# Output weights of an attention layer gated and split earlier and kept in DRAM, and two kinds of vector additions done by accumulating DMAs

## The chip, the cores and the metric

The kernel runs on one core of one Trainium2 chip. The metric is the device time of one launch in microseconds (us); the time of a kernel is the median of several runs. The engines of the core are named as the profile names them: PE is TensorE (matrix products; PEld is its loading of weights), DVE is VectorE, ACT is ScalarE, POOL is GpSimd, SP is SyncE, which here only issues DMAs. Operands lie in SBUF as tiles of 128 partitions, sums of products in PSUM, everything larger in DRAM.

## The reference, cut to what matters

Two layers of a decoder trunk work on x of 1024 rows (SEQ) by 1024 (D_MODEL) in float32. Each layer is a token mixer followed by a squared-ReLU MLP of width 4096; each of the four sub-layers is `x <- LayerNorm(ALPHA * x + gate * f(x * (1 + scale) + shift))`, where shift, scale and gate come from a condition vector. The first mixer is a gated MLP over chunks; the second, which the change is about, is an attention of 16 heads of 64 in three dilated patterns:

```python
B_PATTERNS = ((128, 1), (512, 4), (2048, 16))       # window, dilation
def mixer_b(h, w_qkv, w_out, slopes):
    qkv = (h @ w_qkv).reshape(B, S, N_PAT, 3, B_HEADS, B_HEAD_DIM)
    for g, (window, dilation) in enumerate(B_PATTERNS):
        o, lse = dilated_branch(qkv[:, :, g, 0], qkv[:, :, g, 1], qkv[:, :, g, 2],
                                window, dilation, slopes)
        outs.append(o)
        lses.append(lse)
    wts = jax.nn.softmax(jnp.stack(lses, axis=0), axis=0)[..., None]
    o = jnp.sum(wts * jnp.stack(outs, axis=0), axis=0)
    return o.reshape(B, S, B_HEADS * B_HEAD_DIM).astype(h.dtype) @ w_out
...
        y = mixer_b(h, b_w_qkv[j], b_w_out[j], slopes)
        x = layer_norm(ALPHA * x + gate * y, ln_g[i, 0], ln_b[i, 0])
```

`dilated_branch` is a causal softmax attention inside a window with a linear bias (ALiBi). So per position and head there are three outputs and three log-sums `lse`; the softmax over the three gives the weights with which the outputs are added, and the sum is multiplied with `w_out`.

## The kernel before, in words

**Numbers and products.** A float32 operand is split into a high and a low part that the array takes: `split` (L102, L103) copies to the high part on ACT and forms source minus high part on DVE. Each product is then three matmuls (high by high, high by low, low by high).

**Stages.** After mixer A and its MLP comes `values`, then `attention`, and then the MLP of layer 1. `values` runs over the 35 entries of `V_STEPS`, each a pattern `g`, a kind `X` (0 and 1 are q and k of the undilated pattern g=0, 2 is v) and one of the seven products `p` of a Strassen-like scheme, in the order 1, 2, 5, 6, 7, 4, 3. Each step makes four sums `m` of 12 matmuls each. `evict` (L1215) takes the finished sums: products 1, 5 and 6 are only copied; after the other four the result is split into a tile of pool `parted`, tag `vs`, which has two buffers, and stored by a POOL DMA, q and k to `qk_dram` (L1229), v to `v_dram` (L1234). The right-hand weights of a step are loaded by SP one to two steps ahead (L1099).

**Attention.** `attention` (L1272) treats pairs of heads, 8 of them, and in each pair the patterns 2, 1, 0: 24 groups in a fixed order, with 8 slots each and two positions in a slot. Work is put at a position by `at(slot, position)`; the program is then written out position by position. Between the positions it writes a stream of projections, `project()` (L1358: q and k of the dilated patterns), by a credit. In a group the scores (L1447) get their bias and row maximum in a DVE operation (L1467) and their exponential on ACT (L1469), are transposed (L1500, L1503) and split (pThi on ACT, pTlo on DVE), and a slot and a half later multiplied with v (L1527). The outputs are gathered in a tile `oT`, half by an ACT copy (L1536) and half by a DVE one (L1537); the tag `oT` has four buffers. The biases are made by POOL (L1435), a group ahead.

**Merge.** When the three groups of a pair are done, `merge(hp)` combines them. With `base` the first slot behind the pair's last group, the statistics are read at `base + 1` and made into three rows of factors; at `base + 4`, `spread` loads the factors, broadcast over the partitions, into three tiles `box[g]` (program name `bc`) in the order g = 1, 2, 0 (L1611, six SP DMAs of 256 KB). Then twelve steps follow, one in each slot from `base + 9` to `base + 20`: `scale` multiplies half an `oT` into its `bc` tile (L1623) for g = 2, 1, 0, `add` adds half of `box[2]`, then of `box[1]`, to `box[0]` on DVE (L1627), and `cut` splits `box[0]` by halves into the other two tiles, which SP stores to `o_dram` (L1638). For pair 6 the steps take one position each instead of a slot, and for the last pair they come behind the attention, in `go_on`.

**Affine rows.** The residual of the next layer norm needs eight blocks of 128 rows of `spill[1]`, scaled by a row g and added to a row b. They are loaded during the first groups; `affine_row(i)` (L1678) multiplies and adds on DVE in place and stores the block back by a POOL DMA (L1679).

**Output weights.** `w_out` has eight units of 128 rows. From 15 slots ahead of the last group, `gate_row` loads the gate of the sub-layer into a buffer of the tag `oT`, and `staged_unit(k)` loads a unit raw (L1708, 512 KB on SP), multiplies it by the gate on DVE (L1712) and splits it into two tiles of the tags `whi` and `wlo`, which have four buffers each. Units 0 to 3 are ready before the last group, 4 and 5 near its end, 6 and 7 in `go_on`. `accumulate` (L1756) multiplies with them in five groups of sums: a and b with units 0 to 3 and 0 to 1 beside the last group, c, d and e behind it (units 2 and 3, then 4 to 7 for each half of the rows). Group a and b's sums get the residual rows added by an accumulating DMA on POOL (L1767), the later groups add on DVE (L1769).

**Order.** The framework's planner orders the instructions of an engine by its own reckoning of costs and of when inputs are ready. `tc.keep_in_program_order` (here also `in_order`) ties an instruction only behind the one written just before it on its engine; one that is written later may still pass it. DMAs of SP and of POOL wait in the order of their queue.

## Time and profile before

| what | value |
|---|---|
| median of 3 runs (lowest, highest) | 2727.97 us (2726.43, 2732.16) |
| the profiled execution | 2727.96 us; span 2726.2 us |
| busy PE / PEld | 2658.8 us (98%) / 2196.3 us (81%) |
| busy DVE / ACT / POOL | 1989.8 us (73%) / 1377.1 us (51%) / 97.0 us (4%) |
| DMA | 487.98 MB moved, mean 179 GB/s |

The span runs from the first to the last recorded instruction; the profiled time has 1.8 us around it. In that execution the values' stage ends near 1377 us and the scores of the attention run from 1415 to 2015 us; the five merges of the pairs 0 to 4 start near 1516, 1591, 1668, 1742 and 1816 us, those of the pairs 5 and 6 near 1890 and 1964. The last group of output products (e) ends near 2096 us, and the MLP of layer 1 takes the rest.

### The profile page before, as it was taken

Reading aid. Unit: us, or ns where it says so; the run is one execution under the profiler, and the core shown is the slowest. Engines: PE = TensorE matmul, PEld = TensorE weight load, DVE = VectorE, ACT = ScalarE, POOL = GpSimd, SP = SyncE. Lnnn points to the kernel's source line nnn. Section 1 sums busy time; section 2 is a strip of 40 time slices with the busy share of each in tenths; the row PEclk is TensorE's granted clock in tenths of the full one; section 3 lists DMA queues with packets and bytes.
Section 4 is the critical chain, followed back from the end, with each engine's and each line's share of the span. In section 5 each row is a group of like instructions: output and inputs, shape, how many; then the busy total and the mean of one; then the engine's idle time right before and its main releaser. Section 6 shows DMA issues by size and latency. Waiting matters only on the chain.

```text
span 2726.2 us, 36911 instructions
## 1 busy us (share of the span) xinstructions
PE 2658.8 (98%) x13242; PEld 2196.3 (81%) x13242; DVE 1989.8 (73%) x3594; ACT 1377.1 (51%) x2593; POOL 97.0 (4%) x161
## 2 busy tenths in 40 slices
PE   6999999999999999999999999999999999999998
PEld 5788888887888878888888888888777788878886
DVE  6787698787867778555557767777768966577877
ACT  3354375555443464434436666666655655554332
POOL 1000000000000000111110000000010000000000
PEclk9999999999999999999999999999999999999999
DMA  7534346667936545655565554555672654485562
GB/s 263 159 118 134 116 140 224 227 214 257 333 131 194 195 155 193 212 186 182 178 210 153 155 140 129 132 144 139 193 183 105 202 189 159 149 311 192 171 207 86
DMA packets 332572, 487.98 MB, mean 179 GB/s; under 512 B 50988, under 2 KB 176340, under 8 KB 332388
## 3 DMA queue, kind: packets, MB, share of 16 engines
q1 hardware_dynamic: 318564, 435.29, 50.3%
q0 software_dynamic: 13824, 50.34, 5.2%
q8 instruction: 104, 1.70, 0.3%
q14 instruction: 80, 0.66, 0.1%
HBM read 357.01 MB, written 128.53 MB: 178 GB/s over the span
## 4 chain that ended last, share of the span: by engine, by line
PE 77%; DVE 12%; DMA 6%; ACT 3%; issue 2%; SPq 1%; DVEq 0%; ACTq 0%
PE psd L955 22%; PE psv L1257 13%; PE psua L796 7%; PE psq L1358 6%; PE psk L1358 6%; DMA adaw<-in_ada_w_dram 3%; PE psuc L796 3%; PE psd_wout L389 3%; PE psu L368 3%; PE pv L1527 3%; PE sc L1447 2%; PE psv L470 2%; PE psub L796 2%; DVE adaacc L128 1%; DVE left L103 1%
## 5 line engine op out<-in xcount | busy, mean ns | idle before, releaser
L796 PE MATMUL psua<-right,left 128*128 128x512 f32 x1536 | 363.4, 390 | 0.3
L955 PE MATMUL psd<-rhi,lhi 128*128 128x512 f32 x896 | 349.9, 390 | 3.0 <-ACT part L827 3.0
L955 PE MATMUL psd<-rlo,lhi 128*128 128x512 f32 x896 | 349.6, 390 | 0.2
L955 PE MATMUL psd<-rhi,llo 128*128 128x512 f32 x896 | 349.2, 390 | 0.0
L796 PEld LDWEIGHTS psua<-right,left 128*128 128x128 f32 x1536 | 287.1, 188 | 61.7 <-DVE right L103 1.4
L1469 ACT ACTIVATE p<-p,stat 128x128 f32<-128x128 f32 (+1 forms) x384 | 168.7, 441 | 107.8 <-DVE stat L1467 104.7
L955 PEld LDWEIGHTS psd<-rhi,lhi 128*128 128x128 f32 x896 | 168.6, 188 | 39.1 <-ACT part L827 3.9
L955 PEld LDWEIGHTS psd<-rlo,lhi 128*128 128x128 f32 x896 | 168.5, 188 | 35.9 <-DVE rlo L103 1.1
L955 PEld LDWEIGHTS psd<-rhi,llo 128*128 128x128 f32 x896 | 168.6, 188 | 35.0
L796 PE MATMUL psuc<-right,left 128*128 128x512 f32 x768 | 187.2, 390 | 0.0
L128 DVE SCALAR_TENSOR_TENSOR adaacc<-adaw,silu_c,adaacc 128x512 f32<-128x512 f32 x168 | 128.5, 775 | 55.0 <-DMA adaw<-in_ada_w_dram 54.6
L796 PEld LDWEIGHTS psuc<-right,left 128*128 128x128 f32 x768 | 143.5, 188 | 30.0 <-DVE right L103 0.4
L103 DVE TENSOR_TENSOR pTlo<-pT,pThi 128x512 fp32r<-128x512 f32 (+1 forms) x160 | 99.3, 621 | 75.1 <-ACT pThi L102 74.1
L103 DVE TENSOR_TENSOR left<-ws,left 128x512 fp32r<-128x512 f32 x128 | 87.8, 688 | 71.5 <-ACT left L102 69.7
L103 DVE TENSOR_TENSOR llo<-lraw,lhi 128x1024 fp32r<-128x1024 f32 x112 | 136.4, 1218 | 0.8 <-ACT lhi L102 0.8
L102 ACT CAST left<-ws 128x512 fp32r<-128x512 f32 x128 | 79.1, 620 | 99.1 <-DVE ws L717 87.8
L1358 PE MATMUL psk<-form_L,wqk_hi 128*128 128x512 f32 x384 | 127.0, 412 | 0.0
L1358 PE MATMUL psq<-form_L,wqk_hi 128*128 128x512 f32 x384 | 126.4, 410 | 0.0
L102 ACT CAST rhi<-rraw 128x1024 fp32r<-128x1024 f32 x48 | 50.6, 1053 | 139.6 <-issue 113.7
L1257 PE MATMUL psv<-vrhi,form_S 128*128 128x512 f32 x384 | 119.9, 390 | 0.6 <-ACT vrhi L102 0.4
L102 ACT CAST lhi<-lraw 128x1024 fp32r<-128x1024 f32 x112 | 117.4, 1048 | 3.5 <-PE psua L796 3.5
L1467 DVE CUSTOM_DVE_ANT_0 p<-sc,bias 128x128 f32<-128x128 f32 (+1 forms) x384 | 113.6, 346 | 6.7 <-PE sc L1447 5.8
(326 smaller groups left out, 6094.4 us busy)
## 6 DMA issues: line engine op xcount, KB each, us to landing
lraw<-forms SPq DMA_DIRECT2D x112, 512.0 KB
adaw<-in_ada_w_dram SPq DMA_DIRECT2D x192, 256.0 KB
up<-in_mlp_w_up_dram SPq DMA_DIRECT2D x64, 512.0 KB
forms<-s SPq DMA_DIRECT2D x128, 256.0 KB
rraw<-in_mlp_w_down_dram SPq DMA_DIRECT2D x64, 512.0 KB
forms<-part SPq DMA_DIRECT2D x96, 256.0 KB
v<-vs POOLq DMA_DIRECT2D x48, 512.0 KB, 3.7
vraw<-in_b_w_qkv_dram SPq DMA_DIRECT2D x42, 512.0 KB
```

What stands on the lines that cost most here:

```text
L102: first = A.copy(hi, src) if hi_engine is A else hi_engine.tensor_copy(hi, src)
L103: return first, lo_engine.tensor_tensor(lo, src, hi, op=ALU.subtract)
L128: ins = V.scalar_tensor_tensor(acc[:], raw[:], silu_c[:, k : k + 1], acc[:], ALU.mult, ALU.add)
L368: T.matmul(dst, s[a], m[b], start=(n == 0), stop=(n == last))
L389: T.matmul(p[:], stat[a][:, k, o : o + P], u[b][:, w], start=n == 0, stop=n == count - 1)
L796: T.matmul(acc, w[:, a, k, :], right[p][:, b, k, :], start=p in (1, 2, 5) and k + a + b == 0, stop=k == 3 and a == 1, skip_group_check=True)
L955: ins = T.matmul(sums[kind, m][:], l[a][:, k, m * P : (m + 1) * P], r[b][:, k, :], start=p in (1, 5, 2, 3) and kp + k + a + b == 0, stop=k ...
L1257: T.matmul(acc, rows[:, m * P : (m + 1) * P], cols_, start=p in (1, 2, 5) and kp + k + a + b == 0, stop=kp == 1 and k == 1 and a == 1, ski ...
L1358: T.matmul(p[:], wu[a][:, k * P : (k + 1) * P], h_op(k, half, b), start=k + c_ == 0, stop=k == KD - 1 and c_ == 2)
L1467: V.tensor_tensor_reduce(out=pr, in0=banks[e][:, sl], in1=st["bias"][:, width - w :], scale=-0.125, scalar=3e38, op0=ALU.add, op1=ALU.min, ...
L1469: A.activation(pr, pr, AF.Exp, bias=nm, scale=-1.0, accum_out=l)
L1527: T.matmul(pvs[b][:, q0 % HALF : q0 % HALF + w_], stt, x_[:, o_ : o_ + w_], start=not begun[b], stop=left[b] == 0, skip_group_check=True)
```

## The change

- In `values`, from step (1, 2, 3) on, the two halves of the gate row are held in SBUF. In the steps of pattern 0 with p in 1, 5, 6, in which `evict` stores nothing, 16 pieces (unit k, half dh of its columns) of `w_out` are loaded into a buffer of the tag `vs`, multiplied by the gate on DVE, split, and stored by POOL to a new DRAM tile `wo_dram`.
- In the attention `gate_row` and `staged_unit` are gone. `load_unit(k)` brings both parts of a unit from `wo_dram` with two SP DMAs: units 0 to 5 at position 1 of the slots -15, -14, -12, -9, 8 and 9 from the last group, units 6 and 7 in `go_on` behind group c.
- The merges of pairs 0 to 6 scale g = 0, 2, 1 in the slots `base + 9`, `+ 10`, `+ 11`, both halves in one slot; behind g = 2 and g = 1 an accumulating POOL DMA adds the whole tile to `box[0]` (`gather`), and both halves are cut in slot `base + 16`. The last pair is merged as before.
- The affine rows only multiply on DVE; the row b is stored once to DRAM (`b_row`), and an accumulating POOL DMA adds it, broadcast, to the block, ahead of the block's store. Rows 4 to 7 come at a spacing of six slots instead of five.

```diff
+    wo_dram = dram.tile([N_PAIRS, P, 2, 2, HALF], F32, name="wo_parts")
...
+            gate, pieces, begun = [], deque((k, dh) for k in range(N_PAIRS) for dh in range(2)), deque()
+
+            def gate_halves():
+                for dh in range(2):
+                    gate.append(work.tile([P, HALF], F32, name=f"gate_2_{dh}", tag="h"))
+                    nc.sync.dma_start(gate[dh][:], gate_dram[2, dh * HALF : (dh + 1) * HALF].partition_broadcast(P))
+
+            def piece_load():
+                k, dh = pieces.popleft()
+                t = parted.tile([P, 2, HALF], F32R, name=f"wo_{k}_{dh}", tag="vs")
+                nc.sync.dma_start(t[:, 1].bitcast(F32), b_w_out[0, k * P : (k + 1) * P, dh * HALF : (dh + 1) * HALF])
+                begun.append((k, dh, t))
+
+            def piece_store():
+                k, dh, t = begun.popleft()
+                raw = t[:, 1].bitcast(F32)
+                V.tensor_tensor(raw, raw, gate[dh][:], op=ALU.mult)
+                split(t[:, 0], t[:, 1], raw)
+                nc.gpsimd.dma_start(wo_dram[k, :, dh, :, :], t[:].bitcast(F32))
+
             for n, (g, X, p) in enumerate(V_STEPS):
+                if (g, X, p) == (1, 2, 3):
+                    run(stream)
+                    gate_halves()
...
                     evict(g, X, p, m)
+                    if g == 0 and p in (1, 5, 6):
+                        if m < 2 and pieces:
+                            piece_load()
+                        elif m > 1 and begun:
+                            piece_store()
...
+                def gather(g):
+                    nc.gpsimd.dma_start(box[0][:], box[g][:], accum_op=ALU.add)
+
...
-                pieces = ((scale, 2), (scale, 1), (scale, 0), (add, 2), (add, 1), (cut, 0))
                 if hp == N_PAIRS - 1:
+                    pieces = ((scale, 2), (scale, 1), (scale, 0), (add, 2), (add, 1), (cut, 0))
                     ending["merge"] = [lambda f=f, g=g, half=half: f(g, half) for half in range(2) for f, g in pieces]
                     return
-                steps = [lambda f=f, g=g, half=half: f(g, half) for f, g in pieces for half in range(2)]
-                pace = 2 if hp < N_PAIRS - 2 else 1
-                for n, f in enumerate(steps):
-                    n = pace * n + 18
-                    at(base + n // 2, n % 2)(f)
+                for i, g in enumerate((0, 2, 1)):
+                    for half in range(2):
+                        at(base + 9 + i, half)(lambda g=g, half=half: scale(g, half))
+                    if g:
+                        at(base + 9 + i, 1)(lambda g=g: gather(g))
+                for half in range(2):
+                    at(base + 16, half)(lambda half=half: cut(0, half))
...
+            b_row = dram.tile([1, D], F32, name="b_row")
...
+                nc.gpsimd.dma_start(b_row[:], affine["b"][0:1, :])
...
-                for n, op in (("g", ALU.mult), ("b", ALU.add)):
-                    tc.keep_in_program_order(V.tensor_tensor(t[:], t[:], affine[n][:], op=op))
+                tc.keep_in_program_order(V.tensor_tensor(t[:], t[:], affine["g"][:], op=ALU.mult))
+                nc.gpsimd.dma_start(t[:], b_row[0].partition_broadcast(P), accum_op=ALU.add)
                 nc.gpsimd.dma_start(spill[1][i * P : (i + 1) * P, :], t[:])
...
-                    at(5 * i - 15, 0)(lambda i=i: affine_load(i))
-                at(*((i + 1, 1) if i < 4 else (5 * i - 12, 1)))(lambda i=i: affine_row(i))
+                    at(6 * i - 20, 0)(lambda i=i: affine_load(i))
+                at(*((i + 1, 1) if i < 4 else (6 * i - 18, 0)))(lambda i=i: affine_row(i))
...
-            def gate_row():
-                ending["gate"] = vec.tile([P, D], F32, name="gate_2", tag="oT", bufs=4)
-                nc.sync.dma_start(ending["gate"][:], gate_dram[2].partition_broadcast(P))
-
-            def staged_unit(k, load, gate, ready):
...
-            staged_unit(0, (-14, 0), (-12, 0), (-11, 0))
-            staged_unit(1, (-13, 0), (-11, 1), (-10, 1))
-            staged_unit(2, (-11, 0), (-10, 0), (-9, 0))
-            staged_unit(3, (-10, 1), (-9, 1), (-8, 0))
-            staged_unit(4, (-2, 0), (2, 0), (8, 0))
-            staged_unit(5, (-1, 0), (4, 0), (8, 1))
-            late = [staged_unit(6, (9, 0), (11, 1), None), staged_unit(7, (9, 1), (12, 1), None)]
+            def load_unit(k):
+                ending["units"][k] = tuple(wts.tile([P, D], F32R, name=f"wo_{k}_{m}", tag=f"w{m}")[:] for m in ("hi", "lo"))
+                for i, t in enumerate(ending["units"][k]):
+                    nc.sync.dma_start(t.rearrange("p (d c) -> p d c", c=HALF).bitcast(F32), wo_dram[k, :, :, i, :])
+
+            for k, slot in enumerate((-15, -14, -12, -9, 8, 9)):
+                at(last_group + slot, 1)(lambda k=k: load_unit(k))
...
-                for f in late:
-                    f()
+                for k in (6, 7):
+                    load_unit(k)
```

19 lines of the change are left out of this document (removed).

## The prediction

> **What bounds the kernel now.** I read the page first, then the busy time of every engine in stretches of time, then the single instructions around the merges.
>
> ```profile
> span 2726.2 us, 36911 instructions
> ...
> PE 2658.8 (98%) x13242; PEld 2196.3 (81%) x13242; DVE 1989.8 (73%) x3594; ACT 1377.1 (51%) x2593; POOL 97.0 (4%) x161
> ```
>
> TensorE is busy for 2658.8 of 2726.2 us, so only the 67 us in which it idles, and stretches in which its clock is low, can be won by moving other engines' work. The profiled execution took 2727.96 us, 1.8 us more than its span, and the median of the runs is 2727.97, so a change of the span can be added to the median as it stands. Some 0.2% of that, 5.5 us, is about what a measurement of this kernel tells from no change.
>
> The windows below have, after the stretch and its length, the busy time of PE, PEld, DVE, ACT and POOL, then PE's granted clock, the DMA share and GB/s.
>
> ```profile
> 1042.00:1377.00 335.00, 334.70 (x1476) 277.04 (x1477) 200.14 (x234) 137.95 (x193) 45.45 (x76) 1.00 0.59 202
> 1500.00:1600.00 100.00, 98.06 (x650) 82.16 (x648) 68.70 (x226) 62.21 (x190) 2.97 (x8) 1.00 0.52 138
> 1600.00:1700.00 100.00, 98.89 (x668) 82.33 (x667) 73.84 (x219) 64.09 (x190) 2.98 (x8) 1.00 0.54 146
> 1960.00:1966.00 6.00, 4.45 (x36) 3.65 (x34) 3.60 (x14) 2.65 (x13) 0.00 (x0) 1.00 1.01 262
> 1966.00:1972.00 6.00, 3.45 (x16) 2.90 (x17) 5.40 (x10) 4.74 (x10) 0.00 (x0) 0.77 0.66 257
> 1972.00:1978.00 6.00, 3.95 (x29) 2.95 (x27) 6.00 (x11) 1.98 (x7) 0.00 (x0) 0.94 0.88 283
> 1978.00:1984.00 6.00, 5.74 (x21) 4.61 (x22) 5.97 (x20) 3.16 (x10) 0.91 (x1) 0.72 1.08 386
> 2026.00:2032.00 6.00, 3.86 (x26) 2.99 (x24) 5.53 (x13) 4.85 (x9) 0.85 (x1) 0.89 0.79 160
> 2032.00:2038.00 6.00, 5.93 (x16) 4.82 (x17) 4.65 (x9) 0.58 (x1) 0.00 (x0) 0.54 0.51 139
> 2038.00:2044.00 6.00, 6.00 (x28) 4.95 (x27) 4.69 (x8) 0.00 (x0) 0.00 (x0) 1.00 1.01 246
> ```
>
> In the stage of the values (first row) PE never waits. In the attention two hundreds (1500 to 1700) lose 1.94 and 1.11 us. The loss sits at the end. From 1960 to 1984 PE idles 1.55 + 2.55 + 2.05 + 0.26 = 6.4 us, and its low clock takes busy time times what is missing to 1: 3.45 x 0.23 + 3.95 x 0.06 + 5.74 x 0.28 = 2.6 us; in sum 9.0. DVE is full there (5.97 to 6.00 of 6 in the last two rows of that stretch). From 2026 to 2038 PE idles 2.2 us and then runs at 0.54: 3.86 x 0.11 + 5.93 x 0.46 = 3.2 us; in sum 5.4. So 14.4 us are open there, and what the change does to DVE in the attention is worth something only at these places.
>
> **Output weights out of the attention.** Before, each of the eight units costs a multiplication by the gate and a low half on DVE and a high half on ACT:
>
> ```profile
> L1712 DVE TENSOR_TENSOR wo_raw<-wo_raw,gate x8: 1205/1218/1226, 1952.7 to 2036.2; 128x1024 f32<-128x1024 f32 x8
> L102 ACT CAST wo_hi<-wo_raw x8: 1044/1048/1058, 1953.9 to 2046.5; 128x1024 fp32r<-128x1024 f32 x8
> L103 DVE TENSOR_TENSOR wo_lo<-wo_raw,wo_hi x8: 1203/1216/1225, 1955.0 to 2049.8; 128x1024 fp32r<-128x1024 f32 x8
> ```
>
> That is 1.218 + 1.216 = 2.43 us of DVE and 1.05 us of ACT per unit. Units 0 to 3 are prepared from 1952.7 on, in and just ahead of the full stretch: 9.7 us of DVE leave it. The gate row leaves too, and with it one of the four buffers of the tag `oT` comes free. What that buffer and the scales do there:
>
> ```profile
> 1963.92 1.98 DVE L1623 TENSOR_TENSOR bc<-oT,bc 128x512 f32<-128x512 f32 x2 [1.97 <-DMA bc<-w_dram]
> ...
> 1965.99 1.07 ACT L1536 COPY oT<-pv 64x512 f32<-64x512 f32 x2 [2.69 <-DVE bc L1623]
> ...
> 1966.60 1.28 DVE L1537 TENSOR_TENSOR oT<-oT,pv 64x512 f32<-64x512 f32 x2 [0.70 <-ACT oT L1536]
> ...
> 1967.71 0.33 PE L1527 MATMUL pv<-pThi,v 128*128 128x128 f32 x1 [3.26 <-ACT pThi L102]
> ```
>
> DVE waits 1.97 us for the broadcast factors, multiplies, ACT's copy into a new `oT` waits 2.69 us for that multiplication, and PE waits 3.26 us for what ACT does next. With a fourth buffer ACT needn't wait for the scale. Merge 6 also gives up four additions:
>
> ```profile
> L1623 DVE TENSOR_TENSOR bc<-oT,bc x48: 669/1066/1102, 1516.0 to 2051.5; 128x512 f32<-128x512 f32 x48
> L1627 DVE TENSOR_TENSOR bc<-bc,bc x32: 669/682/691, 1533.0 to 2053.4; 128x512 f32<-128x512 f32 x32
> ```
>
> 4 x 0.682 = 2.7 us, and its two cuts move five slots on. DVE's surplus in this stretch is gone, so most of the 9.0 us should go. What remains depends on the first multiplication (next part): at best a wait like the 0.77 us shown there, so 8.2 us are won. At worst the multiplication starts 2.1 us later, at 1966.05, and two copies of 0.68, the gather (1.28) and a low half (0.68) follow: PE goes on at 1969.4 where it could have gone on at 1967.71 - 3.26 = 1964.45. That leaves 4.9 us and some 1.5 us of low clock, so 2.6 us are won. I take 6.5, nearer to the best, since 12.4 us of DVE work go.
>
> Near 2030 the splits of units 4 and 5 lie between the last halves of the probabilities, one of them here:
>
> ```profile
> 2030.33 1.22 DVE L103 TENSOR_TENSOR wo_lo<-wo_raw,wo_hi 128x1024 fp32r<-128x1024 f32 x1
> ```
>
> Two such (2.4 us of DVE, 2.1 of ACT) leave the stretch in which PE idled 2.2 us. If 1.5 us of idling go and the clock still falls, 1.5 are won; if it doesn't fall, 4.7. I take 4.0. The Trainium skill, page "TensorE: Matmul & The Clock Gate", section "HAM oscillation — how this bites in real kernels", holds that the array falls to half speed after a gap of more than about 3.4 us. The trace differs: 0.54 was granted after 2.2 us of idling in all. By the rule nothing of the 3.2 us would come back, and the sum would be 3 us less; the rows decide.
>
> **Loads of units 6 and 7.** They now come as two halves of 512 KB each, and can't start before the third group of products (`c`) has released units 2 and 3. Before, their splits took ACT and DVE until 2049.8 + 1.2.
>
> ```profile
> L1756 PE MATMUL psod<-wo_hi,oTs x64: 389/389/470, 2046.0 to 2067.6; 128*128 128x512 f32 x64
> ```
>
> `d` begins at 2046.0, and units 2 and 3 are free at about that time. Its 96 products take 21.6 us, 0.225 each. The planner puts the 24 of units 4 and 5 first, as it does now, which covers 5.4 us, to 2051.4; unit 7 is needed 12 products later, at 2054.1. For issue and landing of such a transfer the nearest rows are POOL's (from the DMA issues of the page, 512 KB from the issue to the landing, and from the tile `acc`):
>
> ```profile
> v<-vs POOLq DMA_DIRECT2D x48, 512.0 KB, 3.7
> ```
>
> ```profile
> L1767 POOL DMA_DIRECT2D acc<-spill x8: 837/854/909, 1983.1 to 2026.5; - x8
> ...
> DMA to landing us min/median/max: 5.3/5.5/7.5
> ```
>
> With 0.85 us of issue, 3.7 to land, and every further 512 KB 1.4 to 2.1 us behind the one before (386 and 246 GB/s, rows 1978 and 2038), unit 6 is complete at 2052.0 to 2052.7 and unit 7 at 2054.8 to 2056.9. PE waits 0.6 to 2.8 us; against it, merge 7 finishes earlier since 4.9 us of DVE work (two gates, two low halves) leave. I take +1 (-1 to +3).
>
> **Splitting in the value stage.** Sixteen pieces, half of the above each: 0.6 + 0.6 us of DVE and 0.5 of ACT, in all about 19 and 8 us, in the 21 last of 35 steps. DVE has 135 us free in that stage and ACT 197, beside a PE without idle time. The scarce thing is the tag `vs` with two buffers:
>
> ```profile
> ACT qs L102 <- DMA qk<-qs: 30.4, 13, 4.8
> ```
>
> ACT already waits there for q's and k's stores. A piece holds a buffer from its load to its store, in steps that use none now, and SP's load waits for the buffer with the next values' loads behind it. These are issued a step (48 products, some 11 us) ahead. I take 0 (0 to +3).
>
> **Affine rows.** One DVE addition per row goes, from a stretch where PE has no idle time, so nothing is won. POOL now waits for an accumulate before it stores a row, and the next bias is behind that. POOL makes biases a group ahead. I take 0 (0 to +2).
>
> **Merges.** Six pairs before the last two stretches. The additions removed lie where PE is full. New is the order: g=0 is scaled first, though `spread` still loads the factors in the order 1, 2, 0; and two multiplications a slot instead of one. Now the wait is for g=2's factors:
>
> ```profile
> 1516.02 1.09 DVE L1623 TENSOR_TENSOR bc<-oT,bc 128x512 f32<-128x512 f32 x1 [3.52 <-DMA bc<-w_dram]
> ...
> 1519.35 0.67 DVE L103 TENSOR_TENSOR pTlo<-pT,pThi 128x512 fp32r<-128x512 f32 x1
> ...
> 1520.08 0.33 PE L1527 MATMUL pv<-pTlo,v 128*128 128x128 f32 x1 [0.77 <-DVE pTlo L103]
> ```
>
> DVE stands 3.52 us for it, and the low half behind it comes 0.77 us late for PE. In the fifth merge it ends at 1819.33, 0.92 us before PE is there:
>
> ```profile
> 1818.65 0.68 DVE L103 TENSOR_TENSOR pTlo<-pT,pThi 128x512 fp32r<-128x512 f32 x1
> ...
> 1820.25 0.23 PE L1527 MATMUL pv<-pThi,v 128*128 128x128 f32 x1
> ```
>
> Factors of g=0 are 2 x 256 KB behind those of g=2: 2.1 us at 246 GB/s. Two copies of 0.68 instead of one of 1.07 add 0.3. If DVE's order stays as written, PE waits 0.77 + 2.4 = 3.2 us in the first merge and 2.4 - 0.92 = 1.5 in the fifth; six of their mean make 14, less the 3.05 idle today: +11. But the pin ties a multiplication only behind what was written before it; what was written later may pass if the planner's costs have it ready sooner. A broadcast further back gives the gather and the low half of slot 34 a better chance to pass. Then no PE wait hangs on the factors: -3. I take +2: nearer to that end, since the row shows DVE with nothing else to do for 3.5 us, in which these two come ready.
>
> The second half of a merge is two accumulates in a chain on POOL, priced by the rows of `acc` above: 0.85 + 5.5 twice is 12.7 us. A slot is (1963.92 - 1516.02) / 144 = 3.1 us, six merges being 144 slots, and the cut stands five slots behind the last multiplication's: 15.5 us of cover, so nothing is added; at 7.5 us to landing it is 16.7, and ACT and DVE wait. The Trainium skill, page "DMA: Bandwidth & Descriptors", section "Anatomy of one DMA — SWDGE (gpsimd) path", gives 2.0 us + bytes / 436 GB/s, 3.2 us for 512 KB: two would take 8.1 us and this risk would be nil. The trace's 5.5 us is for a source in DRAM; I keep it.
>
> **Sum.** -6.5 - 4.0 + 1 + 0 + 0 + 2 = -7.5: 2727.97 - 7.5 = 2720.5 us.
>
> **Rivals.** *The first multiplication stalls each merge.* The order stays as written: +11 at the merges, and only 2.6 won in the last: 11 - 2.6 - 4 + 1 = +5.4, 2733.4; where stalls of 2 to 3 us also drop the clock as they do near 1966 (1.5 us for some three of them), 2738. For it: in the first merge the multiplication, pinned, did stand ahead of all else. Against: the gap has room for others to pass. It decides once factors land more than about 3.5 us after DVE is free, the fifth merge's margin being 0.92.
>
> *Accumulates land late.* At 7.5 us or more, with DVE's backlog, each cut holds ACT 2 to 3 us, and PE has less than 1 us to spare: 7 x 1.9 = +13, in all 2733.5. Against: a source in SBUF, and light DMA traffic there.
>
> *Transfers eat the end.* 1 MB per unit instead of 0.5 joins a DMA system at 1.01 and 1.08 in two of the rows: with 2 won instead of 6.5, nothing near 2030 and 3 lost at unit 7: +3, 2731.
>
> *All merges gain.* If everything passes the multiplications: -3 - 8.2 - 4.5 + 0 = -15.7, 2712.
>
> **How the numbers follow.** Forecast 0.42 (own range 2715 to 2726): 0.31 faster by over 5.5 us, 0.11 within. Stalled merges 0.22: 0.17 slower, 0.05 within. Late accumulates 0.10: 0.07 and 0.03. Transfers 0.08, within. All merges gain 0.18, faster. Together faster 0.49, same 0.27, slower 0.24. A range of 2711 to 2738 leaves out some of the best case and the worst of the stalled ones.
>
> **What would show it.** Right: in 1960 to 1984 PE idles under 3 us at a clock near 1, no ACT copy waits for a multiplication, the clock near 2035 is above 0.9, PE's waits in 1500 to 1900 stay under 6 us, and the value stage stays full. Wrong: PE waits for low halves at every third group of eight slots with DVE waiting for `bc`; ACT waiting for a DMA at the cuts; `psod` waiting for unit 6 or 7; POOL's bias late in the first eight slots.

## The result and the profile after

The changed kernel takes 2827.45 us (median of 6 runs, 2821.48 to 2832.43) against 2729.11 us before on the same chip: 1.0358 times, 95% interval 1.0343 to 1.0373. Forecast was 2720.5 us, with a range to 2738. The change loses 98 us.

The head of the page of the changed kernel:

```profile
span 2825.8 us, 37101 instructions
...
PE 2695.5 (95%) x13242; PEld 2215.0 (78%) x13242; DVE 1966.6 (70%) x3574; ACT 1374.7 (49%) x2601; POOL 121.5 (4%) x200
```

DVE has 23 us less to do, as intended (1989.8 before), and PE idles for 130 us of the span in place of 67. PE's busy time has grown by 37 us at the same 13242 recorded products: the mean granted clock has fallen from 0.995 to 0.98. Where the time went is read from the first and the last start of three groups of instructions: the products of the values (`psv`) and the bias operation `p<-sc,bias`, the first and the last step of the attention. Their rows in the changed kernel, which give first and last start in us:

```profile
L1281 PE MATMUL psv<-vrhi,form_L x288: 388/389/498, 990.7 to 1218.3; 128*128 128x512 f32 x144
L1281 PE MATMUL psv<-form_S,vrlo x128: 387/389/628, 1256.5 to 1397.6; 128*128 128x512 f32 x128
L1496 DVE CUSTOM_DVE_ANT_0 p<-sc,bias x384: 273/292/426, 1445.3 to 2117.0; 128x128 f32<-128x128 f32 x104, 128x256 f32<-128x256 f32 x88
```

So the values take 1397.6 - 990.7 = 406.9 us, the way from there to the first bias operation 47.7, the attention 671.7. The same rows of the kernel before give 385.6, 40.1 and 597.8. The table holds these differences for the profiled execution of each kernel (tail: from the last bias operation to the last product `psoe`; the values start at 988 to 996 us, in e17 at 1012, and what follows the tail takes 629 to 632). The ratios are those of all runs, each against runs of the kernel before on the same chip; the experiments below are named by the first part of their label.

| kernel | ratio (95% interval) | values | to first bias | attention | tail |
|---|---|---|---|---|---|
| before | 1 | 385.6 | 40.1 | 597.8 | 80.7 |
| after | 1.0358 (1.0343-1.0373) | 406.9 | 47.7 | 671.7 | 78.8 |
| e1_cut_pinned | 1.0128 (1.0112-1.0143) | 407.8 | 47.3 | 607.9 | 78.8 |
| e20_merge_mended | 1.0072 (1.0059-1.0084) | 406.3 | 48.9 | 590.6 | 78.4 |
| e2_merge_only | 1.0254 (1.0231-1.0278) | 386.1 | 40.1 | 671.0 | 80.2 |
| e7_merge_pin_spread | 0.9977 (0.9968-0.9986) | 387.2 | 40.1 | 593.8 | 80.5 |
| e8_merge_dve_adds | 1.0099 (1.0084-1.0115) | 386.2 | 40.1 | 628.1 | 80.7 |
| e4_affine_only | 0.9985 (0.9975-0.9995) | 386.1 | 40.6 | 595.6 | 80.8 |
| e18_merge_affine | 0.9990 (0.9980-1.0000) | 385.6 | 40.1 | 595.5 | 82.0 |
| e3_wo_only | 1.0063 (1.0038-1.0088) | 405.9 | 46.5 | 588.9 | 79.4 |
| e5_wo_res | 0.9988 (0.9977-0.9999) | 396.2 | 40.1 | 590.8 | 79.3 |
| e6_wo_res_affine | 1.0000 (0.9989-1.0010) | 398.9 | 40.4 | 590.4 | 78.4 |
| e10_wo_late | 1.0023 (1.0012-1.0034) | 399.2 | 40.1 | 591.9 | 78.4 |
| e11_wo_late_merge | 1.0001 (0.9992-1.0010) | 398.5 | 40.2 | 589.8 | 79.0 |
| e12_all_mended | 1.0018 (1.0009-1.0027) | 400.6 | 41.2 | 589.3 | 78.9 |
| e14_wo_late_pinned | 1.0068 (1.0054-1.0082) | 411.7 | 41.5 | 590.8 | 78.8 |
| e15_wo_late_pinned_pool | 1.0084 (1.0072-1.0097) | 412.7 | 42.9 | 591.5 | 78.7 |
| e16_with_merges | 1.0064 (1.0051-1.0077) | 409.1 | 41.7 | 589.3 | 78.7 |
| e17_no_buffers | 1.0045 (1.0028-1.0063) | 386.9 | 40.1 | 593.1 | 79.0 |
| e19_no_buffers_stores | 1.0003 (0.9994-1.0012) | 398.1 | 40.1 | 591.5 | 78.9 |

What happens in the attention is seen in the first merge. The timelines of DVE, POOL, ACT and PE there, one engine behind the other (start, length, engine, line, operation, and in brackets the idle time before it and what ended it):

```profile
1553.47 3.01 DVE L1652 TENSOR_TENSOR bc<-oT,bc 128x512 f32<-128x512 f32 x3
...
1560.07 0.86 POOL L1655 DMA_DIRECT2D bc<-bc  x1 [4.22 <-DVE stat L1496]
...
1557.62 0.48 ACT L102 CAST pThi<-pT 128x384 fp32r<-128x384 f32 x1
1567.85 0.62 ACT L102 CAST bc<-bc 128x512 fp32r<-128x512 f32 x1 [9.74 <-DMA bc<-bc]
1568.37 0.40 ACT L1498 ACTIVATE p<-p,stat 128x128 f32<-128x128 f32 x1
...
1571.63 0.69 DVE L1566 TENSOR_TENSOR oT<-oT,pv 64x512 f32<-64x512 f32 x1 [11.11 <-ACT oT L1565]
...
1568.91 0.48 PE L1529 MATMUL pT<-ident,p 128*128 128x128 f32 x1 [4.96 <-ACT p L1498]
```

The last multiplication of this merge is the third of those from 1553.47 on, which end at 1556.5. The second accumulate goes out at 1560.07. ACT has taken the high half of the cut next in its row, right behind a high part of probabilities at 1557.62, and stands 9.74 us until the accumulate has landed. Behind it stand the exponentials that everything needs: DVE idles 11.11 us, PE 4.96. The clock follows. Two windows behind each other (columns as before):

```profile
1560.00:1570.00 10.00, 5.04 (x27) 4.08 (x26) 0.52 (x6) 2.15 (x8) 1.68 (x3) 0.79 0.64 157
1570.00:1580.00 10.00, 8.41 (x31) 5.92 (x30) 4.75 (x14) 5.52 (x18) 0.00 (x0) 0.50 0.29 77
```

The other six merges do the same. ACT's waits over the attention, with their sum, number and longest:

```profile
ACT bc L102 <- issue: 36.9, 4, 10.6
...
ACT bc L102 <- DMA bc<-bc: 17.6, 2, 9.7
ACT oTs L102 <- DMA bc<-bc: 7.1, 1, 7.1
```

That is 61.6 us in seven stands. ("issue" where the profile saw no releaser: the place in the row is the same.)

### The profile page after: what moved, and what is told of

It is laid out like the page before. It is cut to its first block, busy times and chain, and to the rows that moved or that the text cites. A ratio compares the mean times of both kernels' runs of the same rounds, so it can differ in the third digit from the quotient of the medians.

```text
span 2825.8 us, 37101 instructions
## 1 busy us (share of the span) xinstructions
PE 2695.5 (95%) x13242; PEld 2215.0 (78%) x13242; DVE 1966.6 (70%) x3574; ACT 1374.7 (49%) x2601; POOL 121.5 (4%) x200
## 4 chain that ended last, share of the span: by engine, by line
PE 60%; issue 14%; DVE 12%; DMA 8%; ACT 4%; POOL 2%; SPq 1%; POOLq 0%; DVEq 0%; ACTq 0%
PE psd L955 21%; PE psua L796 7%; PE psk L1387 5%; PE psq L1387 4%; PE psuc L796 3%; DMA adaw<-in_ada_w_dram 3%; PE psd_wout L389 3%; PE psu L368 3%; PE pv L1556 2%; PE sc L1476 2%; PE psub L796 2%; PE psv L470 1%; DVE adaacc L128 1%; DMA bc<-bc 1%; DVE left L103 1%
## 5 line engine op out<-in xcount | busy, mean ns | idle before, releaser
L1387 PE MATMUL psk<-form_L,wqk_hi 128*128 128x512 f32 x384 | 136.3, 438 | 4.7 <-DVE qlo L103 4.7
L1566 DVE TENSOR_TENSOR oT<-oT,pv 64x512 f32<-64x512 f32 x96 | 65.7, 684 | 100.0 <-ACT oT L1565 99.3
```

The source lines that it names most:

```text
L1387: T.matmul(p[:], wu[a][:, k * P : (k + 1) * P], h_op(k, half, b), start=k + c_ == 0, stop=k == KD - 1 and c_ == 2)
L1566: V.tensor_tensor(dst, dst, pvs[b][main, :], op=ALU.add)
```

## The experiments

**The cut** (e1). `split` gives back two instructions, and only the second, DVE's low half, is tied to its place. This ties both:

```diff
-                    in_order(split(hi, lo, box[0][:, w])[1])
+                    for x_ in split(hi, lo, box[0][:, w]):
+                        in_order(x_)
```

> The changed kernel with one edit: in the cut of a merge, the high half on ACT is pinned behind what was written before it, as the low half on DVE is already, so that it stays five slots behind the last multiplication. Theory A, early cut: in the changed kernel ACT takes the high half at once behind the last multiplication and stands 7 to 10.6 us for the second accumulate, seven times, and this is most of the loss in the attention (73.9 us between the first and the last bias operation). Then this kernel comes back by 60 to 75 us, to 2755 to 2770, and ACT's waits for the cut (54.6 us) nearly vanish. Rival B, slow accumulates: the two accumulates in a chain take longer than the five slots (15.5 us), or hold POOL and the DMA engines, wherever the cut stands: then less than 25 us come back. Rival C, first multiplication: the loss is DVE's wait for the factors (25.8 us in 7): then nothing comes back.

Measured 2766.07 us, 1.0128: by the medians 61 us come back, and the attention shrinks by 63.8 us (671.7 to 607.9). ACT's long stands are gone; what is left in the first merge is the wait for the factors, on DVE and then on PE:

```profile
1550.26 1.29 DVE L1652 TENSOR_TENSOR bc<-oT,bc 128x512 f32<-128x512 f32 x2 [6.48 <-DMA bc<-w_dram]
...
1554.54 0.47 PE L1556 MATMUL pv<-pTlo,v 128*128 128x128 f32 x1 [3.61 <-DVE pTlo L103]
```

So theory A holds and B falls: five slots do cover two accumulates, but for 2.9 us that ACT still waits at two of the cuts. Their landing in the changed kernel, from the tile `bc`:

```profile
L1655 POOL DMA_DIRECT2D bc<-bc x14: 838/861/903, 1555.0 to 2081.9; - x14
...
DMA to landing us min/median/max: 4.4/5.0/7.7
```

**The merges alone** (e2), without the other parts of the change.

> The kernel before with the new merges alone (order 0, 2, 1, accumulates, cut in slot 16). Theory A: these carry the loss in the attention, so about 2729 + 74 = 2803, with ACT standing 7 to 10 us at each cut. If instead the affine rows or the loads of the output weights share in it, clearly less, under 2780.

Measured 2800.99, 1.0254; the attention takes 671.0 us, the same as in the full change. The other parts add nothing to this loss; nor do the 8.9 us that the output weights alone win in the attention (e3 in the table) show in the full change.

**DVE additions in the place of the accumulates** (e8), at the same positions, with nothing pinned:

```diff
-                        at(base + 9 + i, 1)(lambda g=g: gather(g))
+                        [at(base + 9 + i, 1)(lambda g=g, half=half: add(g, half)) for half in range(2)]
```

> The kernel before with the new merges alone, order 0, 2, 1 and cut in slot 16 as changed and nothing pinned, but the two accumulates replaced by the four DVE additions, written in their places. Theory A says that ACT's wait in the cut is the landing of the accumulates, which the planner reckons far too early: with DVE additions ACT no longer stands there (under 1 us each), and only the first multiplication's 10 us are left: 2735 to 2742. If the order 0, 2, 1 or the place of the cut is the trouble itself, the kernel stays near 2800.

Measured 2759.25, 1.0099. ACT's stand at the cut is gone; what is left there is short, and for a DVE addition:

```profile
ACT bc L102 <- DVE bc L1630: 12.8, 6, 2.8
```

ACT still takes the high half early: in the first merge at 1527.73, right behind the last addition, and DVE's low half, which is tied, comes at 1538.81. But here what it reads is ready early too. This is what theory A said of the accumulates, if not under 1 us each. What the planner reckons for a transfer stands in no trace; the rows show only where it puts the copy. But 2735 to 2742 was a miss: the attention is 30 us longer than before, not 10. The six multiplications and four additions now lie in three slots, and a low half of the probabilities comes behind them:

```profile
1522.91 1.05 DVE L1623 TENSOR_TENSOR bc<-oT,bc 128x512 f32<-128x512 f32 x1
1523.88 1.27 DVE L1630 TENSOR_TENSOR bc<-bc,bc 128x512 f32<-128x512 f32 x2
1525.08 2.02 DVE L1623 TENSOR_TENSOR bc<-oT,bc 128x512 f32<-128x512 f32 x2
1527.02 1.27 DVE L1630 TENSOR_TENSOR bc<-bc,bc 128x512 f32<-128x512 f32 x2
1528.22 0.68 DVE L103 TENSOR_TENSOR pTlo<-pT,pThi 128x512 fp32r<-128x512 f32 x1
```

A part of the 30 us is the wait for the factors, whose order is the old one here (DVE waits 22.7 us for them in seven). No run has the additions together with both repairs, so what the accumulates themselves are worth was not measured.

**The order of the factors** (e7). On the merges alone, with the pinned cut, the loads are put into the order of use:

```diff
-                    for g in (1, 2, 0):
+                    for g in ((0, 2, 1) if hp < N_PAIRS - 1 else (1, 2, 0)):
```

> The kernel before with the new merges alone, the high half of the cut pinned, and the factors of pairs 0 to 6 loaded in the order in which they are used, 0, 2, 1. Theory C, first multiplication: what the pinned cut left over in the attention (10 us against before, and 19 against the output weights alone, PE standing up to 3.6 us behind DVE's wait of 6.5 us for the factors) is the wait for factors that are loaded last. Then the merges cost nothing any more: 0.996 to 1.002 of before. Rival F, accumulates: POOL's DMAs and their traffic cost it, and the order of the loads changes nothing: 1.004 to 1.007.

Measured 2725.90 against 2729.85, 0.9977 (0.9968 to 0.9986). The loss is gone and a small gain shows: the attention takes 593.8 us. PE's waits for low halves over the attention, first of the merges alone (e2), then of this kernel:

```profile
PE pv L1527 <- DVE pTlo L103: 16.0, 18, 3.9
```

```profile
PE pv L1527 <- DVE pTlo L103: 4.6, 7, 1.4
```

This run differs from e2 by the pin and by the order; the next one differs from e1 by the order alone.

**Both repairs in the changed kernel** (e20).

> The changed kernel with the two repairs of the merges only (high half pinned, factors in the order of use); weights and affine rows as changed. The pinned cut brought it to 2766. With the wait for the factors gone too, the attention takes 588 to 592 us in place of 607.9 and 671.7, and what is left over before is the values' loss of 21 + 7.6 us less the 10 won at the end: 2744 to 2751, 1.005 to 1.008.

Measured 2748.34, 1.0072. The attention falls from e1's 607.9 to 590.6 us, 7 us under that of the kernel before, and DVE's waits for the factors from 26.3 us in seven to 4.0 in three. So theory C holds for what the pin had left. What remains is the values' stage: 20.7 and 8.8 us lost there, 9.5 won behind it, 3.1 from the later start of the stage in this execution: 23.1 against a span longer by 2749.1 - 2726.2 = 22.9. So every part of the 98 us has its stage; what makes the loss in the values' stage is the question of the runs that follow.

**The output weights alone** (e3).

> The kernel before with the output weights alone: pieces in the stage of the values, units loaded from DRAM. Theory D: the pieces hold the two buffers of the tag vs, SP's loads of them wait for the stores, DVE and ACT wait for these loads, PE loses some 21 us by the end of that stage and 4.7 us just behind it; in the attention's end up to 7 us come back: 2729 + 21 + 5 - 7 = 2748 (2738 to 2758). Rival: the stage of the values loses by the affine change's POOL DMAs (b_row) or by the gate's two tiles; then this kernel's values stage is full and it runs at 2720 to 2727.

Measured 2746.78, 1.0063. The end of the attention won what the prediction said. The two stretches that it named, shifted as the merge of pair 6 (its first multiplication starts at 1986.88, before at 1963.92) and the end of the scores are (columns as before, first and third row before, second and fourth e3):

```profile
1960.00:1984.00 24.00, 17.59 (x101) 14.10 (x100) 20.97 (x53) 12.53 (x37) 0.91 (x1) 0.86 0.91 297
```

```profile
1983.00:2007.00 24.00, 21.73 (x139) 18.01 (x138) 16.59 (x50) 14.20 (x45) 3.12 (x4) 1.00 0.99 307
```

```profile
2026.00:2038.00 12.00, 9.79 (x42) 7.81 (x41) 10.18 (x20) 5.42 (x10) 0.85 (x1) 0.72 0.65 149
```

```profile
2040.00:2052.00 12.00, 10.66 (x61) 8.83 (x60) 8.09 (x22) 4.12 (x9) 0.84 (x1) 1.00 0.98 253
```

Of the 9.0 us lost in the first stretch 2.3 remain, of the 5.4 in the second 1.3, at full clock. The 2.3 us are a new wait, for a unit that comes from `wo_dram`:

```profile
PE psoa L1755 <- DMA wo_hi<-wo_parts: 2.3, 1, 2.3
```

The stage of the values loses 20.3 us and the way to the first bias 6.4. Waits of DVE and of SP's queue there in the changed kernel:

```profile
DVE wo L1254 <- DMA wo<-in_b_w_out_dram: 52.6, 13, 7.3
```

```profile
SPq L1248 <- DMA qk<-qs: 32.9, 7, 14.6
SPq L1248 <- DMA v<-vs: 21.6, 6, 6.9
```

A piece's load waits on SP for q's, k's or v's store to leave the buffer; DVE, which takes its work in order, waits for the load; ACT waits for DVE, and PE for their sums. One such chain in the changed kernel, from the timelines of SP, DVE, ACT and PE:

```profile
1277.34 0.33 SPq L1248 DMA_DIRECT2D wo<-in_b_w_out_dram  x1
...
1283.41 0.69 DVE L1254 TENSOR_TENSOR wo<-wo,gate 128x512 f32<-128x512 f32 x1 [5.30 <-DMA wo<-in_b_w_out_dram]
...
1284.18 0.62 ACT L102 CAST wo<-wo 128x512 fp32r<-128x512 f32 x1 [6.36 <-DVE wo L1254]
...
1287.94 0.73 PE L1281 MATMUL psv<-form_S,vrhi 128*128 128x512 f32 x2 [3.46 <-ACT vpart L1220]
```

Here the load went out 0.8 us before DVE was free, and DVE stood for the transfer itself. By the timelines of SP and DVE some 12 of the 52.6 us lie ahead of the issue of a load, while SP stood for a buffer or for what its queue has before, and some 41 behind it, while the load was under way: 2.6 to 7.4 us from the issue to the multiplication. Of the 7.6 us behind the stage, 4.7 are one stand of PE; ahead of it ACT stands 5.3 us for a store of q or k to leave one of the same two buffers.

**Other buffers for the pieces** (e5).

```diff
-                t = parted.tile([P, 2, HALF], F32R, name=f"wo_{k}_{dh}", tag="vs")
+                t = work.tile([P, 2, HALF], F32R, name=f"wo_{k}_{dh}", tag="res", bufs=3)
```

> The kernel before with the output weights alone, as in the run of the output weights alone, but with the sixteen pieces in the three buffers of the tag res, which nothing else uses in that stage, in place of the two of vs. Theory D, ring: the pieces' cost in the stage of the values (17.8 us at its last product and 6.4 us more to the first bias operation) comes from their holding vs, so that SP's load waits for a store's landing and DVE for the load. Then nearly all of it goes: the stage is as long as before within 4 us, and the 10 us won in the attention stay: 0.996 of the kernel before, about 2720. Rival E, traffic: the pieces' 16 MB of DMA and their 27 us of DVE and ACT work are the cost, whatever buffers they use: then 1.004 to 1.006, as in the run before.

Measured 0.9988 (0.9977 to 0.9999): half of the stage's loss and all of the 6.4 us behind it are gone (396.2 and 40.1 us). The expectation rested on a mistake, found later: `res` is not free in this stage, since `raw_tile` (L657) deals out three of every five weight tiles from it. So SP's loads of the values' weights now wait for the pieces' stores:

```profile
SPq L1100 <- DMA wo_parts<-wo: 72.5, 9, 11.0
```

DVE still stands 33.5 us in eleven for the pieces' loads. (The pieces move 12 MB, 4 in and 8 out, not the 16 of rival E.) Two runs built on this one, first e6:

> The same and the affine rows of the change. They gave 0.9985 (0.9975 to 0.9995) alone. If both gains are of separate places they add: 0.9945, about 2715. If the affine gain was chance, as the run with pieces in res alone.

Measured 1.0000 (0.9989 to 1.0010): the affine rows add nothing here.

The next (e10) multiplies and stores a piece one storeless step after its load (`piece_store` ahead of `piece_load` at m 0 and 1):

> As the run with the pieces in the tag res, but each piece is multiplied, split and stored one of the storeless steps after its load (at m 0 and 1 of the next such step, where before it was two m later in the same step, some 5 us). Theory D, second part: of the values' loss with own buffers (9.7 us at the last product) the rest is DVE standing for the pieces' loads (27.4 us, 8 times) that are issued only two m ahead; then the stage is as long as before within 2 us and this runs at 0.995 to 0.997 of the kernel before, about 2718. Rival E, traffic or the mere work: unchanged at 0.999.

Measured 1.0023: worse, with 399.2 us for the values. The planner had drawn the multiplications forward again, to some 3 to 9 us behind the issue of their loads (the median is near 5), and DVE stood for these as before:

```profile
DVE wo L1254 <- DMA wo<-in_b_w_out_dram: 37.6, 12, 6.7
```

**The same with the merges mended** (e11, e12), without and with the affine rows of the change:

> The run before this with the mended merges (high half pinned, factors loaded in the order of use). Mended merges alone gave 0.9977. The gains overlap near 1960 to 1984, where both free DVE: with 0.9965 for the weights alone, 0.994 to 0.996 together, 2714 to 2719. If the merges' accumulates meet the loads of the units, no better than the weights alone.

> The changed kernel with all three repairs: pieces in res and stored a step later, high half of the cut pinned, factors in the order of use; the affine rows as changed. The affine rows alone gave 0.9985, with the pieces in res nothing: as the kernel without them, within 0.15%, 0.993 to 0.996. If all three places were understood, this is the forecast of 2720 or better, 100 us below the changed kernel.

Measured 1.0001 (0.9992 to 1.0010) and 1.0018 (1.0009 to 1.0027), so 97 and 93 us under the changed kernel and not under the kernel before. The merges' gain comes on top of the run with the weights alone (1.0023 to 1.0001); the attention takes 589.8 and 589.3 us, the values 398.5 and 400.6. Of the three places (the cut, the order of the factors, the values' stage) only the last was not understood.

**Pinned multiplications, and POOL for the loads** (e14, e15, e16). On the late version the multiplication is tied (`tc.keep_in_program_order`), then the load is issued by `nc.gpsimd` in place of `nc.sync`, then the mended merges are added.

> The kernel before with the output weights alone, pieces in res, stored a storeless step after their load, and now the multiplication by the gate pinned behind what is written before it on DVE. In the run without the pin DVE took the multiplications some 5.5 us behind the issue of their loads, not a step later, and stood 31.5 us for them in nine: theory G, the planner draws them forward, as it drew the cut. Then DVE's wait for these loads falls under 10 us, the last product of the values comes at 1377 to 1382 in place of 1390.7, and the kernel runs at 0.995 to 0.998. Rival H, queue: SP stands in order for the pieces' buffers (57.5 us of waits of the values' own loads behind the pieces' stores), so the values' loads stay late: then 1.000 to 1.003.

> The same with the pieces' loads issued by POOL, so that SP's loads of the values wait for no piece. By theory G alone it runs like the run before it; by rival H the loss goes only here: 0.995 to 0.998, with the last product of the values at 1377 to 1381. If neither moves it, the cost is DVE's and ACT's added work and the 16 MB themselves.

> The same and the mended merges (high half of the cut pinned, factors in the order of use). They gave 0.9977 alone and 0.9978 on top of the weights (1.0001 against 1.0023). If they add again: 0.993 to 0.996, 2711 to 2719, the fastest of all.

Measured 1.0068, 1.0084 and 1.0064 (1.0051 to 1.0077): all misses. DVE's wait for the pieces is gone, as theory G said, but now it waits for the weights of the values, and SP, which loads these, for the pieces' buffers of `res`. Rows of e14, from the waits of DVE and of SP's queue:

```profile
DVE v_t L1108 <- DMA vraw<-in_b_w_qkv_dram: 17.8, 3, 8.1
DVE vraw L1111 <- DMA vraw<-in_b_w_qkv_dram: 13.6, 4, 8.0
DVE vraw L1113 <- DMA vraw<-in_b_w_qkv_dram: 9.5, 4, 4.4
```

```profile
SPq L1100 <- DMA wo_parts<-wo: 42.0, 8, 16.4
```

The stage takes 411.7 us. The three waits of DVE come to 40.9 us in eleven; in e10 the waits for these weights were 16.6 in five. So the wait has moved to the values' weights, which share the ring. That the pieces' stores make it is argued and not shown: SP's wait for them is shorter here than it was in e10 (75.4 us in ten), where the stage was shorter too. With POOL's queue for the pieces' loads the stage takes 412.7, so SP's queue is not what costs.

**Work without buffers** (e17, e19).

```diff
+                V.tensor_tensor(t, t, other, op=ALU.max)     # t, other: the gate's two tiles
+                A.copy(t, t)
+                V.tensor_tensor(t, t, other, op=ALU.max)
```

> The kernel before with the output weights alone, where a piece costs the same two DVE operations, one ACT copy and 768 KB of DMA less a third, at the same places, but holds no buffer: DVE and ACT work on the gate's tile in place, and POOL copies the raw weights from DRAM to DRAM twice (gating and splitting are left out, so the weights are raw). The tag res turned out to hold values' weights too (three of every five raw tiles), so the runs with the pieces in res had not freed them of a shared ring. Theory D: the loss of the values' stage is the rings, vs or res, in which pieces, weights and stores wait for one another. Then the last product of the values comes at 1376 to 1381 and the kernel runs at 0.995 to 0.997. Rival E: DVE's and ACT's work and the DMA's traffic are the cost: 1.000 to 1.006, the stage 10 us or more longer.

The whole is 1.0045, but by no wait in this stage: the copies hung on nothing, and the planner put them into the first 55 us of the program, where the stage of the values begins 20.8 us later for it. The work itself was drawn to 1081 to 1147 us, early in the stage (the change has it from 1162 to 1363), which takes 386.9 us: 16 times 0.69 + 0.69 us of DVE and 0.62 of ACT, 22 and 10 us in all, are hidden, as the prediction had it.

> In the run without buffers the copies from DRAM to DRAM hung on nothing and were drawn to the first 55 us of the program, where they cost 20 us; the stage of the values, left with DVE's and ACT's work alone, had no wait of PE and was as long as before (386.9 against 385.6 us). Here the traffic is put back in its place: a piece is the same DVE and ACT work in place on the gate's two tiles and two POOL stores of 256 KB from them (the loads, 256 KB a piece, the gating and the splitting are left out, so the weights are not the reference's). Theory D, shared buffers: the stage stays at 385 to 389 us and the kernel runs at 0.995 to 0.997. Rival E, traffic: the stores' 8 MB make the landing of q's, k's and v's stores late: 392 us or more, over 0.998.

Measured 1.0003, a miss for theory D as it was put: the stage takes 398.1 us. But here too the planner drew the work forward, to 1056 to 1148 us, and the gate's two tiles became a ring of their own, for whose stores DVE stands:

```profile
DVE gate L1251 <- DMA wo_parts<-gate: 16.5, 5, 5.2
```

PE idles 8.0 us between 1056 and 1170 us and nothing after, when the stores are done. In these two runs the work alone is free, and work that stands in DVE's row for a transfer is not. What the traffic alone costs in this stage was not separated from it, and no run gives the pieces a ring of their own; so rival E is weakened and not excluded.

**The affine rows**, alone (e4) and with the mended merges (e18).

> The kernel before with the affine rows alone (one multiplication on DVE, accumulate and store on POOL). POOL stood 34.7 us for these accumulates in the changed kernel, beside biases that are made ahead: 2729, within 4 us. Rival: the 7.6 us lost between the last product of the values and the first bias operation are its doing (biases late): then 2733 to 2737.

> The kernel before with the mended merges (0.9977 alone) and the affine rows of the change (0.9985 alone), which meet nowhere: 0.996 to 0.998, 2717 to 2724, the fastest correct version here. If the affine rows' gain was chance, 0.9977 again.

Measured 0.9985 (0.9975 to 0.9995) and 0.9990 (0.9980 to 1.0000). Alone they look like a gain of 4 us; on top of three other versions the ratio is 0.0012 to 0.0017 higher with them (e6 against e5, e12 against e11, and, on another chip, e18 against e7). Whether they win or cost a few us stays open; the rival, late biases, falls (40.6 us to the first bias operation against 40.1).

## Why the prediction was wrong

*Output weights out of the attention* (-6.5 and -4.0): the sizes are right. The windows give 9.0 - 2.3 = 6.7 us and 5.4 - 1.3 = 4.1. But what is left of the first stretch is PE's 2.3 us for a loaded unit, for which the sum had nothing at this place, and not a wait behind the factors; that the size fits so well is in part luck. (Merge 6's cuts move two slots on by the code, from `base + 14` to `base + 16`, not five; no term rests on it.) *Units 6 and 7* (+1, -1 to +3): a little better than its bounds, the tail is 1.3 us shorter with the weights alone. Attention and tail together won 8.9 + 1.3 = 10.2 us where the sum had 9.5.

*Splitting in the value stage* (0, up to +3): this step failed. It named the scarce thing, the two buffers of `vs`, and quoted ACT's 30.4 us of waits for q's and k's stores (the 43.8 us in 21 for v's stores, at the same buffers, it left out), and then took the price from DVE's and ACT's free time in sum. The work, 22 and 10 us where it had 19 and 8, is hidden in e17. But free time in sum isn't free time in an engine's row: DVE stood 52.6 us for loads, the lesser part before these went out and the greater while they were under way. Measured: 21.3 us in the stage and 7.6 behind it. What of this is the ring, what the early place of the multiplications and what the traffic stays open.

*Merges* (+2, up to +11): this step failed most. The words "the cut stands five slots behind the last multiplication's: 15.5 us of cover" are untrue of ACT's half of the cut. The prediction itself had said that what isn't pinned may pass; it used that for the work behind a multiplication and not for the cut, whose high half the code leaves unpinned. The trace of the kernel before already shows it, in the first merge: ACT's high half stands right behind its addition, and DVE's low half, which is tied, 5.6 us later.

```profile
1540.74 0.62 ACT L102 CAST bc<-bc 128x512 fp32r<-128x512 f32 x1 [1.30 <-DVE bc L1627]
...
1546.30 0.68 DVE L103 TENSOR_TENSOR bc<-bc,bc 128x512 fp32r<-128x512 f32 x1
```

There it waits 1.3 us, for an addition; behind an accumulate it waited 7 to 11. That is 63.8 us. The rival of late accumulates had the right place (ACT standing at the cut) with the wrong condition, a landing of 7.5 us or more, and a fifth of the price: the landing was 5.0 at the median, much as the sum assumed.

*First multiplication*: the rival was right and the forecast wrong. With the cut mended the attention takes 607.9 us, with the factors in the order of use too 590.6: a stall of 17 us, where +11 was written for it. DVE's order stayed as written; the low half didn't pass.

*Affine rows* (0, up to +2): not settled. Alone the runs give -4 us, on top of other versions +3 to +5.

The two pages of the Trainium skill: the rule of "TensorE: Matmul & The Clock Gate", section "HAM oscillation — how this bites in real kernels", that half speed follows a gap of more than some 3.4 us, agrees with the merges, where 0.50 was granted after PE's gap of 4.96 us. The 0.54 before, after 2.2 us in four gaps of which the longest is 0.95 us, is outside it, and the 3.2 us that by the rule would stay lost came back in e3, where the stretch ran at 1.00. The 3.2 us for 512 KB that were estimated from the fit of "DMA: Bandwidth & Descriptors", section "Anatomy of one DMA — SWDGE (gpsimd) path", stand against 5.0 measured for an accumulate from SBUF to SBUF (4.4 at least); the trace's figure was the one to keep.

## What to carry to other kernels

When an operation on an engine is replaced by a DMA, look for every instruction that reads the DMA's result and isn't tied to its place: the planner may set that reader at the head of an engine's row, as here, and all that stands behind it waits for the landing. Look in the trace of before whether such a reader already stands ahead of its place. Price a hidden step by its engine's row and its ring of buffers (who waits for the load, who for the buffer), not by the engine's free time in a stage. Load factors in the order in which they are used.

## What the runs showed that was not expected

Seven stands of some 7 to 11 us on ACT cost 63.8 us of the attention, about 9.1 each. Not all of that is PE standing still. The attention in the changed kernel and in e1, where the cut is tied (columns as before):

```profile
1445.00:2117.00 672.00, 618.06 (x3916) 510.45 (x3913) 391.03 (x1246) 371.80 (x1121) 43.56 (x79) 0.94 0.58 152
```

```profile
1447.00:2055.00 608.00, 589.92 (x3919) 493.21 (x3917) 390.44 (x1243) 370.76 (x1119) 43.47 (x79) 0.99 0.64 168
```

PE idles 53.9 us in the one and 18.1 in the other, 36 us more; the other 28 us are the same products taking longer, at a granted clock of 0.94 in place of 0.99. So these stands cost 1.8 times the time that PE stood still. No version here beats the kernel before by more than the mended merges do, 0.9977 (0.9968 to 0.9986), a gain of 4 us.
